# Eight experts of a mixture layer: one store for seven outputs, one load for six inputs

## The chip, the cores and the metric

The kernel runs on one core of a Trainium2 chip. The metric is the device time of one execution in microseconds (us), as the median of repeated runs. A profile is a record of one execution by the hardware profiler; its span runs from the first to the last instruction and is a little shorter than the time of that execution.

Five engines run side by side and wait for each other on semaphores: TensorE (PE in the profile, with PEld for its weight loads), VectorE (DVE), ScalarE (ACT), GpSimd (POOL) and SyncE (SP). Transfers between the chip's memory (DRAM) and the on-chip memory (SBUF) are issued by an engine and carried out by 16 DMA engines.

## What is computed

Each of 8 experts has an input of 256 rows and two weight matrices. The inputs and outputs are float32.

```python
n_experts, capacity, hidden, expert_hidden = 8, 256, 512, 2048
x:  (n_experts, capacity, hidden)
w1: (n_experts, hidden, expert_hidden)
w2: (n_experts, expert_hidden, hidden)

def reference(x, w1, w2):
    h = np.matmul(x, w1)
    h = np.maximum(h, 0)
    return np.matmul(h, w2).astype(np.float32)
```

A weight matrix is 4.19 MB in DRAM, so the sixteen of them are 67.1 MB; all of x is 4.19 MB, and so is the output.

## The kernel before

**Transfers.** Weights, and x of experts 2 to 7, are loaded by DMAs that POOL issues and that cast from float32 to bfloat16 on the way (`load_w1`, L80; `load_w2`, L84; `load_x`, L72). x of experts 0 and 1 is loaded by SP as float32 and cast by VectorE (`load_x_first`, L65). Each of the two weight pools has four buffers, so an expert's weights can only be loaded once the weights of the expert four places before have been used. A weight matrix is one DMA, but for those in `PIECES` (L55): w2 of expert 6 comes in two halves, w2 of expert 7 in a half and two quarters. x of experts 2 and 3, of 4 and 5 and of 6 and 7 come in one load each (`X_GROUPS`, L61), into the two buffers of `xb2`, so that the third waits until expert 3 has been transposed.

**Computation of one expert.** `prepare` (L114) transposes x on TensorE, 8 blocks of 128 by 128, and VectorE copies the result out of PSUM. `layer1` (L127) multiplies with w1 in 64 matmuls of 128x128 by 128x256; ScalarE applies the maximum with 0 after every 8 of them. `layer2` (L149) multiplies with w2 in 32 matmuls of 128x128 by 128x512, into two PSUM tiles, which VectorE copies to the output tile. For an expert in `PIECES` the loop over the rows of w2 is the outer one, so that the first matmuls need only the first piece; for the others the two halves of the output rows come one after the other. The last copy of expert 7 is on ScalarE.

**Stores.** The outputs are gathered in groups (`GROUPS`, L58). `store` (L91) writes a group with one DMA from POOL: experts 0 to 2 in the middle of the kernel, experts 3 to 6 (`DEFER`, L60) just ahead of the second layer of expert 7. Expert 7 is stored from SP (L174), after its last copy.

**Order.** TensorE and POOL run in the order in which the program is written (L178). POOL's is: w1 of 0, identity matrix, w2 of 0, the identity matrix a second time (L184), x of 2 and 3, then w1 and w2 by turns, with x of 4 and 5 behind w2 of 2, and x of 6 and 7 behind w2 of 4. At the end of the list w1 of 7 is put ahead of w2 of 6 (L104). `issue` (L106) only decides at which place of the program a load is written; on POOL that sets the order among loads and stores. The first store stands behind w1 of 7 and ahead of w2 of 6 (L192 to L194). TensorE's order is, for each expert, first layer, transposes of the next expert, second layer; in the last round the first layer of expert 7 comes ahead of the second layer of expert 6 (L197).

The trace shows POOL's issues running ahead of the transfers: eight are in flight, and the ninth is issued at 15.32 us, when the first weights have landed.

Of the kernel before, what the change touches and what calls it, by code (L numbers as in the profile page):

```python
# [10 lines left out]
BF16 = mybir.dt.bfloat16  # L11
# [3 lines left out]
def kernel(  # L15
# [7 lines left out]
    nc = tc.nc  # L23
    P = 128
    E, C, H = x.shape
    F = w1.shape[2]
    MC = C // P
    K1 = H // P
# [5 lines left out]
    xg_v = x.rearrange("e (p mo) k -> p e (mo k)", mo=MC)  # L34
# [4 lines left out]

    const = ctx.enter_context(tc.tile_pool(name="const", bufs=1))  # L40
    x_pool = ctx.enter_context(tc.tile_pool(name="x_pool", bufs=2))
    xb_pool = ctx.enter_context(tc.tile_pool(name="xb_pool", bufs=2))
    xT_pool = ctx.enter_context(tc.tile_pool(name="xT_pool", bufs=2))
    w1_pool = ctx.enter_context(tc.tile_pool(name="w1_pool", bufs=4))
    w2_pool = ctx.enter_context(tc.tile_pool(name="w2_pool", bufs=4))
# [6 lines left out]
    identity = const.tile([P, P], BF16, name="identity")  # L52


    PIECES = {E - 2: [8, 8], E - 1: [8, 4, 4]}  # L55


    GROUPS = [(0, 1, 2), (3, 4, 5, 6), (7,)]  # L58
    GROUP = {e: g for g in GROUPS for e in g}
    DEFER = GROUPS[-2]  # L60
    X_GROUPS = [(2, 3), (4, 5), (6, 7)]  # L61

    xbs, w1s, w2s, outs = {}, {}, {}, {}

    def load_x_first(e):  # L65
        t = x_pool.tile([P, MC * H], FP32, name="x_sb")
        nc.sync.dma_start(t[:], x_v[e])
        b = xb_pool.tile([P, MC, P, K1], BF16, name="xb")
        nc.vector.tensor_copy(b[:].rearrange("p m q k -> p (m q k)"), t[:])  # L69
        xbs[e] = b[:]  # L70

    def load_x(g):  # L72
        t = xb_pool.tile([P, 2, MC, P, K1], BF16, name="xb2")
        nc.gpsimd.dma_start(  # L74
            t[:].rearrange("p e m q k -> p e (m q k)"), xg_v[:, g[0]:g[0] + 2, :]
        )
        for i, e in enumerate(g):
            xbs[e] = t[:, i]
# [5 lines left out]
    def load_w2(e):  # L84
        w2s[e] = t = w2_pool.tile([P, K2 * H], BF16, name="w2_sb")
        k = 0
        for n in PIECES.get(e, [K2]):
            nc.gpsimd.dma_start(t[:, k * H:(k + n) * H], w2_v[e, :, k * H:(k + n) * H])  # L88
            k += n

    def store(g):  # L91
        nc.gpsimd.dma_start(  # L92
            og_v[:, g[0]:g[-1] + 1, :], outs[g][:].rearrange("p e m h -> p e (m h)")
        )

    loads = []
    for e in range(E):
        for g in X_GROUPS:  # L100
            if g[0] == e + 1:
                loads.append((load_x, g))
        loads += [(load_w1, e), (load_w2, e)]
    loads[-3], loads[-2] = loads[-2], loads[-3]  # L104

    def issue(upto):  # L106
        while loads:
            f, e = loads[0]
            if (f, e) not in upto:
                break  # L110
            loads.pop(0)
            f(e)

    def prepare(e):  # L114
        xb = xbs[e]
        xt_ps = psum_t.tile([P, K1, MC, P], BF16, name="xt_ps")
        for ko in range(K1):
            for mo in range(MC):
                nc.tensor.transpose(xt_ps[:, ko, mo, :], xb[:, mo, :, ko], identity[:])  # L119
        xT = xT_pool.tile([P, K1, C], BF16, name="xT")  # L120
        nc.vector.tensor_copy(  # L121
            xT[:].rearrange("p k c -> p (k c)"),
            xt_ps[:].rearrange("p k m q -> p (k m q)"),
        )
        return xT

    def layer1(e, xT):  # L127
        w1_r = w1s[e][:].rearrange("p (ko q j) -> p ko q j", ko=K1, j=K2)
        hT = hT_pool.tile([P, K2, C], BF16, name="hT")
        for pr in range(K2 // 2):  # L130
            h_ps = psum_h.tile([P, 2, C], FP32, name="h_ps")
            for s in range(2):
                j = pr * 2 + s
                for ko in range(K1):
                    nc.tensor.matmul(  # L135
                        h_ps[:, s, :],
                        w1_r[:, ko, :, j],
                        xT[:, ko, :],
                        start=(ko == 0),
                        stop=(ko == K1 - 1),  # L140
                    )
            nc.scalar.activation(  # L142
                hT[:, pr * 2:pr * 2 + 2, :].rearrange("p a c -> p (a c)"),
                h_ps[:].rearrange("p a c -> p (a c)"),
                mybir.ActivationFunctionType.Relu,
            )
        return hT

    def layer2(e, hT):  # L149
        last = e == E - 1  # L150
        g = GROUP[e]
        if e == g[0]:
            outs[g] = out_pool.tile([P, len(g), MC, H], FP32, name=f"out_sb{g[0]}")
        out_sb = outs[g][:, e - g[0]]
        o_ps = [psum_o.tile([P, H], FP32, name="o_ps") for _ in range(MC)]
        if e in PIECES:
            order = [(k, m) for k in range(K2) for m in range(MC)]
        else:
            order = [(k, m) for m in range(MC) for k in range(K2)]
        for k, m in order:  # L160
            nc.tensor.matmul(  # L161
                o_ps[m][:],
                hT[:, k, m * P:(m + 1) * P],
                w2s[e][:, k * H:(k + 1) * H],
                start=(k == 0),
                stop=(k == K2 - 1),
            )
            if k == K2 - 1:
                if last and m == 1:
                    nc.scalar.copy(out_sb[:, m, :], o_ps[m][:])  # L170
                else:
                    nc.vector.tensor_copy(out_sb[:, m, :], o_ps[m][:])  # L172
        if last:
            nc.sync.dma_start(out_v[e], out_sb.rearrange("p m h -> p (m h)"))  # L174

    load_x_first(0)
    load_x_first(1)
    with tc.manual_schedule(engines={mybir.EngineType.PE, mybir.EngineType.Pool}):  # L178
        f, e = loads.pop(0)
        f(e)  # L180
        make_identity(nc, identity)
        f, e = loads.pop(0)
        f(e)
        make_identity(nc, identity)  # L184
        issue([(load_w2, 0), (load_x, X_GROUPS[0]), (load_w1, 1), (load_w2, 1), (load_w1, 2)])
        xT = prepare(0)
        for e in range(E - 1):
            issue(
                [(load_w2, e + 2), (load_w1, e + 3), (load_w1, E - 1), (load_w2, e + 1)]
                + [(load_x, g) for g in X_GROUPS if g[0] <= e + 4]  # L190
            )
            for g in GROUPS[:-2]:  # L192
                if g[-1] == e - 1:
                    store(g)  # L194
            hT = layer1(e, xT)
            xT = prepare(e + 1)
            if e == E - 2:  # L197
                hT_last = layer1(E - 1, xT)
            layer2(e, hT)
        store(DEFER)  # L200
        layer2(E - 1, hT_last)
# [1 line left out]
_INS = ['x', 'w1', 'w2']  # L203
_OUTS = [((8, 256, 512), 'float32')]
# [25 lines left out]
```

## Time and profile before

| what | value |
|---|---|
| median of 5 runs | 182.54 us (182.26 to 182.87) |
| the profiled execution | 182.26 us |
| its span | 180.5 us |
| mean granted TensorE clock | 0.949 |
| read from memory / written to it | 71.30 MB / 4.19 MB |
| share of the packets of POOL's queue (q0) in 16 engines' span | 97.6% |
| TensorE idle ahead of first-layer matmuls, waiting for weights | 35.8 us |
| TensorE idle ahead of second-layer matmuls, waiting for weights | 9.1 us |
| POOL's wait for a free x buffer | 26.4 us |
| POOL's wait of the second store for VectorE's copy | 37.7 us |

The GB/s of the profile count bytes as they are written, so that a weight counts half of what is read. The chain of waits lists the work that ended last in order of time: start, duration, engine and what it computes. `h_ps L135` is a first layer, `o_ps L161` a second layer, `xt_ps L119` the transposes.

When TensorE starts again after a wait for weights, these have just landed. The starts in the trace:

| expert | first layer starts | second layer starts |
|---|---|---|
| 0 | 15.07 | 24.77 |
| 1 | 37.99 | 47.67 (no wait) |
| 2 | 57.41 | 67.04 |
| 3 | 79.22 | 88.96 |
| 4 | 98.62 | 108.82 |
| 5 | 120.50 | 130.16 |
| 6 | 139.85 | 158.74, second half 163.60 |
| 7 | 150.21 | 168.47 |

A first layer takes 7.21 us at the full clock; where TensorE had been idle for 4.57 us or more it took 8.88 to 9.35 us, and the clock that the profile shows fell to half meanwhile.

### The profile page before, as it was taken

The numbers are of one execution on the slowest core, as the hardware profiler recorded it, in microseconds if no ns is written. First come the engines' busy times: TensorE is split into PE (matmuls) and PEld (weight loads), VectorE is DVE, ScalarE is ACT, GpSimd is POOL, SyncE is SP. The second block draws the span as 40 slices with busy tenths as digits, with TensorE's granted clock in tenths as the row PEclk, the third lists the DMA queues.
The fourth block names the chain that finished last, engine by engine and source line by source line (L and its number), as shares of the span: only waits on it lengthen the run. The fifth ranks groups of instructions, "written<-read, shape, count | busy, mean of one in ns | idle before, by whom it ended". The sixth has DMA issues, their size and how long they took to land.

```text
span 180.5 us, 1859 instructions
## 1 busy us (share of the span) xinstructions
PE 125.9 (70%) x832; PEld 89.0 (49%) x832; DVE 17.1 (9%) x25; ACT 40.1 (22%) x66; POOL 15.3 (8%) x32
## 2 busy tenths in 40 slices
PE   0206999059994959449994958629994967887790
PEld 0105964049742944138842954228841967833330
DVE  1300011100111011100111010200111010000210
ACT  2001630014400730005500640004500553600000
POOL 7601011010000031000200002010100000000100
PEclk9999999957999999957999999997999999999998
DMA  6999999999999989989998999999899989999995
GB/s 235 230 232 192 214 232 211 196 232 232 196 211 232 229 167 244 232 174 232 232 229 178 232 193 221 225 232 229 182 229 232 218 189 365 218 214 215 209 390 213
DMA packets 4919, 40.48 MB, mean 224 GB/s; under 512 B 432, under 2 KB 432, under 8 KB 2736
## 3 DMA queue, kind: packets, MB, share of 16 engines
q0 software_dynamic: 4480, 38.80, 97.6%
q1 hardware_dynamic: 432, 1.57, 2.3%
q8 instruction: 6, 0.10, 0.2%
q14 instruction: 1, 0.01, 0.0%
HBM read 71.30 MB, written 4.19 MB: 418 GB/s over the span
## 4 chain that ended last, share of the span: by engine, by line
PE 60%; DMA 19%; another core or an unknown queue 16%; POOL 1%; issue 1%; ACT 0%; POOLq 0%
PE h_ps L135 31%; PE o_ps L161 27%; DMA w_sb<-in_w_dram 19%; PE xt_ps L119 1%; POOL xb L74 0%; POOL w_sb L82 0%; ACT out_sb L170 0%; POOL identity masks.py:199 0%; POOL identity masks.py:197 0%; POOL w_sb L88 0%; POOLq masks.py:199 0%; POOLq L214 0%
## 5 line engine op out<-in xcount | busy, mean ns | idle before, releaser
L135 PE MATMUL h_ps<-xT,w_sb 128*128 128x256 bf16 x512 | 65.2, 294 | 35.8 <-DMA w_sb<-in_w_dram 35.8
L135 PEld LDWEIGHTS <-w_sb 128*128 128x128 bf16 x512 | 60.0, 148 | 42.5 <-DMA w_sb<-in_w_dram 39.1
L142 ACT ACTIVATE hT<-h_ps 128x512 bf16<-128x512 f32 x64 | 38.2, 597 | 117.8 <-PE h_ps L135 117.8
L161 PE MATMUL o_ps<-w_sb,hT 128*128 128x512 bf16 x256 | 56.7, 379 | 9.1 <-DMA w_sb<-in_w_dram 9.1
L161 PEld LDWEIGHTS <-hT 128*128 128x128 bf16 x256 | 25.0, 98 | 38.8 <-issue 10.5
L172 DVE COPY out_sb<-o_ps 128x512 f32<-128x512 f32 x15 | 10.3, 691 | 65.1 <-PE o_ps L161 65.1
L121 DVE COPY xT<-xt_ps 128x1024 bf16<-128x1024 bf16 x8 | 5.5, 690 | 89.3 <-PE xt_ps L119 89.3
L88 POOL DMA_DIRECT2D w_sb<-in_w_dram x11 | 5.9, 536 | 57.9 <-DMA w_sb<-in_w_dram 56.2
L119 PE MATMUL xt_ps<-identity,xb 128*128 128x128 bf16 x64 | 5.3, 230 | 4.8 <-DVE xb L69 4.8
L82 POOL DMA_DIRECT2D w_sb<-in_w_dram x8 | 4.7, 584 | 31.5 <-PE h_ps L135 18.4
L119 PEld LDWEIGHTS <-xb 128*128 128x128 bf16 x64 | 4.7, 117 | 4.7 <-DVE xb L69 4.7
L92 POOL DMA_DIRECT2D out_dram<-out_sb x2 | 1.5, 756 | 37.9 <-DVE out_sb L172 37.7
L170 ACT COPY out_sb<-o_ps 128x512 f32<-128x512 f32 x1 | 0.6, 585 | 17.5 <-PE o_ps L161 17.5
L74 POOL DMA_DIRECT2D xb<-in_x_dram x3 | 2.1, 716 | 26.4 <-PE xt_ps L119 26.4
L69 DVE CAST xb<-x_sb 128x1024 bf16<-128x1024 f32 x2 | 1.4, 698 | 4.5 <-DMA x_sb<-in_x_dram 4.5
L142 ACT ACT_TABLE_LOAD x1 | 1.3, 1283 | 0.7 <-PEq L214 0.7
masks.py:199 POOL TENSOR_SCALAR_AFFINE_SELECT identity<-identity 128x128 bf16<-128x128 bf16 x2 | 0.6, 287 | 0.2
masks.py:197 POOL MEMSET identity<- 128x128 bf16 x2 | 0.4, 224 | 0.0
L214 POOL MEMSET const-float32-0.0<- 128x1 f32 x1 | 0.1, 98 | 0.2 <-issue 0.2
L214 POOL MEMSET const-bfloat16-1.0<- 128x1 bf16 x1 | 0.1, 101 | 0.0
L214 POOL MEMSET const-uint8-127<- 128x1 uint8 x1 | 0.1, 101 | 0.0
L214 POOL MEMSET const-float32-1.0<- 128x1 f32 x1 | 0.1, 98 | 0.0
## 6 DMA issues: line engine op xcount, KB each, us to landing
w_sb<-in_w_dram POOLq DMA_DIRECT2D x14, 2048.0 KB, 61.2
w_sb<-in_w_dram POOLq DMA_DIRECT2D x3, 1024.0 KB, 57.2
out_dram<-out_sb POOLq DMA_DIRECT2D x1, 2048.0 KB, 9.8
xb<-in_x_dram POOLq DMA_DIRECT2D x3, 512.0 KB, 45.4
out_dram<-out_sb POOLq DMA_DIRECT2D x1, 1536.0 KB, 64.4
x_sb<-in_x_dram SPq DMA_DIRECT2D x2, 512.0 KB, 3.6
w_sb<-in_w_dram POOLq DMA_DIRECT2D x2, 512.0 KB, 46.6
out_dram<-out_sb SPq DMA_DIRECT2D x1, 512.0 KB, 3.4
```

Of the source, the lines that this page charges most:

```text
L69: nc.vector.tensor_copy(b[:].rearrange("p m q k -> p (m q k)"), t[:])
L74: nc.gpsimd.dma_start(t[:].rearrange("p e m q k -> p e (m q k)"), xg_v[:, g[0]:g[0] + 2, :])
L82: nc.gpsimd.dma_start(w1s[e][:], w1_v[e])
L88: nc.gpsimd.dma_start(t[:, k * H:(k + n) * H], w2_v[e, :, k * H:(k + n) * H])
L92: nc.gpsimd.dma_start(og_v[:, g[0]:g[-1] + 1, :], outs[g][:].rearrange("p e m h -> p e (m h)"))
L119: nc.tensor.transpose(xt_ps[:, ko, mo, :], xb[:, mo, :, ko], identity[:])
L121: nc.vector.tensor_copy(xT[:].rearrange("p k c -> p (k c)"), xt_ps[:].rearrange("p k m q -> p (k m q)"),)
L135: nc.tensor.matmul(h_ps[:, s, :], w1_r[:, ko, :, j], xT[:, ko, :], start=(ko == 0), stop=(ko == K1 - 1),)
L142: nc.scalar.activation(hT[:, pr * 2:pr * 2 + 2, :].rearrange("p a c -> p (a c)"), h_ps[:].rearrange("p a c -> p (a c)"), mybir.ActivationF ...
L161: nc.tensor.matmul(o_ps[m][:], hT[:, k, m * P:(m + 1) * P], w2s[e][:, k * H:(k + 1) * H], start=(k == 0), stop=(k == K2 - 1),)
L170: nc.scalar.copy(out_sb[:, m, :], o_ps[m][:])
L172: nc.vector.tensor_copy(out_sb[:, m, :], o_ps[m][:])
```

## The change

x of experts 2 to 7 is loaded in one DMA, behind w2 of expert 0, into a buffer of its own; the pool of these tiles has one buffer per name. The first seven outputs form one group, which is stored behind the second layer of expert 6. Loads go by turns to the end: w1 of 6, w2 of 6, w1 of 7, w2 of 7. w2 of expert 6 is one DMA, w2 of expert 7 two halves, and so expert 6 takes the other loop order in its second layer. The first layer of expert 7 stands behind the second layer of expert 6 and the store. The identity matrix is made once.

```diff
-    xb_pool = ctx.enter_context(tc.tile_pool(name="xb_pool", bufs=2))
+    xb_pool = ctx.enter_context(tc.tile_pool(name="xb_pool", bufs=1))
...
-    PIECES = {E - 2: [8, 8], E - 1: [8, 4, 4]}
+    PIECES = {E - 1: [8, 8]}
...
-    GROUPS = [(0, 1, 2), (3, 4, 5, 6), (7,)]
+    GROUPS = [tuple(range(E - 1)), (E - 1,)]
     GROUP = {e: g for g in GROUPS for e in g}
-    DEFER = GROUPS[-2]
-    X_GROUPS = [(2, 3), (4, 5), (6, 7)]
+    X_GROUPS = [tuple(range(2, E))]
...
-        b = xb_pool.tile([P, MC, P, K1], BF16, name="xb")
+        b = xb_pool.tile([P, MC, P, K1], BF16, name=f"xb{e}")
...
     def load_x(g):
-        t = xb_pool.tile([P, 2, MC, P, K1], BF16, name="xb2")
+        t = xb_pool.tile([P, len(g), MC, P, K1], BF16, name="xbs")
         nc.gpsimd.dma_start(
-            t[:].rearrange("p e m q k -> p e (m q k)"), xg_v[:, g[0]:g[0] + 2, :]
+            t[:].rearrange("p e m q k -> p e (m q k)"), xg_v[:, g[0]:g[-1] + 1, :]
         )
...
-    loads[-3], loads[-2] = loads[-2], loads[-3]
...
         make_identity(nc, identity)
-        f, e = loads.pop(0)
-        f(e)
-        make_identity(nc, identity)
         issue([(load_w2, 0), (load_x, X_GROUPS[0]), (load_w1, 1), (load_w2, 1), (load_w1, 2)])
         xT = prepare(0)
         for e in range(E - 1):
             issue(
-                [(load_w2, e + 2), (load_w1, e + 3), (load_w1, E - 1), (load_w2, e + 1)]
+                [(load_w2, e + 2), (load_w1, e + 3), (load_w2, e + 1)]
                 + [(load_x, g) for g in X_GROUPS if g[0] <= e + 4]
             )
-            for g in GROUPS[:-2]:
-                if g[-1] == e - 1:
-                    store(g)
             hT = layer1(e, xT)
             xT = prepare(e + 1)
-            if e == E - 2:
-                hT_last = layer1(E - 1, xT)
             layer2(e, hT)
-        store(DEFER)
-        layer2(E - 1, hT_last)
+        store(GROUPS[0])
+        hT = layer1(E - 1, xT)
+        layer2(E - 1, hT)
```

## The prediction

> **What bounds the kernel now.** I read the page's engine shares first, then its DMA rows, then the chain of waits with its times, then the windows of the last ten microseconds.
>
> ```profile
> PE 125.9 (70%) x832; PEld 89.0 (49%) x832; DVE 17.1 (9%) x25; ACT 40.1 (22%) x66; POOL 15.3 (8%) x32
> DMA  6999999999999989989998999999899989999995
> out_dram<-out_sb POOLq DMA_DIRECT2D x1, 2048.0 KB, 9.8
> out_dram<-out_sb POOLq DMA_DIRECT2D x1, 1536.0 KB, 64.4
> out_dram<-out_sb SPq DMA_DIRECT2D x1, 512.0 KB, 3.4
> ```
>
> TensorE idles for 30% of the span, the DMA engines only in the last slice. So the kernel is a stream of bytes with a tail, and only three things can move its end: the length of the stream, what is left after the last weights, and how well the tail is filled.
>
> ```profile
> 130.16 7.07 PE o_ps L161 x32
> 137.23 2.58 another core or an unknown queue
> 139.81 0.05 issue
> 139.85 7.21 PE h_ps L135 x64
> 147.06 0.45 PE xt_ps L119 x8
> ...
> 150.21 7.21 PE h_ps L135 x64
> 157.42 1.27 another core or an unknown queue
> ...
> 158.74 3.61 PE o_ps L161 x16
> ...
> 163.60 3.61 PE o_ps L161 x16
> ...
> 168.47 7.08 PE o_ps L161 x32
> ```
>
> The "unknown queue" pieces are waits for weights, as the page's groups name them for these lines, so each start after one dates a landing: w2 of expert 5 at 130.16, w1 of 6 at 139.85, w1 of 7 at 150.21, the halves of w2 of 6 at 158.74 and 163.60, the first half of w2 of 7 at 168.47. Starts that lie one whole weight apart (57.41 to 67.04, 79.22 to 88.96, 88.96 to 98.62, 120.50 to 130.16, 130.16 to 139.85 in the same view) give 9.63 to 9.74, mean **9.68 us a weight**; a half takes 4.86 or 4.87. The last quarter so lands near 168.47 + 4.87 = 173.34.
>
> ```profile
> 170.00:171.00 1.00, 1.00 (x6) 0.47 (x5) 0.00 (x0) 0.00 (x0) 0.00 (x0) 1.00 1.00 201
> 171.00:172.00 1.00, 1.00 (x7) 0.47 (x5) 0.00 (x0) 0.00 (x0) 0.00 (x0) 1.00 1.04 266
> 173.00:174.00 1.00, 1.00 (x6) 0.49 (x5) 0.00 (x0) 0.00 (x0) 0.00 (x0) 1.00 1.06 434
> 174.00:175.00 1.00, 1.00 (x7) 0.45 (x5) 0.00 (x0) 0.00 (x0) 0.00 (x0) 1.00 0.99 410
> 175.00:176.00 1.00, 0.54 (x3) 0.04 (x1) 0.64 (x1) 0.43 (x1) 0.00 (x0) 1.00 1.03 426
> 176.00:177.00 1.00, 0.00 (x0) 0.00 (x0) 0.05 (x1) 0.16 (x1) 0.00 (x0) 1.00 0.72 295
> 178.00:179.00 1.00, 0.00 (x0) 0.00 (x0) 0.00 (x0) 0.00 (x0) 0.00 (x0) 1.00 0.56 229
> ```
>
> The last number is GB/s written. With the three windows left out (348, 410, 12) the ten add to 3.03 MB after 170.0; the two stores in there are 2.62 MB, so 0.41 MB is weights, 1.92 us at the 213 of the windows before. The store phase therefore starts at **171.93**, runs at a mean of 423 in its middle, and ends where 229 runs out, 178.0 + 229/423 = 178.54, call it 178.57 with the last 12. Without loss it would have ended at 171.93 + 2.62/0.423 = 178.12; most of the 0.45 lost is the window of 295, (423 - 295)/423 = 0.30: the big store runs dry and the last one, issued at 176.19, is not yet flowing. The last store lands at 176.19 + 3.40 = 179.59, 1.02 after its bytes; 0.91 later the span ends.
>
> **The change, part by part.**
>
> *The store of experts 0 to 2 leaves the stream.* From w1 of 6 to the first half of w2 of 6 it is 158.74 - 139.85 = 18.89 us; less w1 of 7 (9.68) and the half (4.86) leaves 4.35 for this store, 362 GB/s for its 1.573 MB. At the 423 of the tail it would be 3.72. The last weights land 4.35 us earlier (3.72 at least, if its turnarounds stay), at 168.99.
>
> *It comes back in the tail.* 3.67 MB go out behind the last weights, and 0.52 MB from SP: 4.194 MB / 0.423 = 9.92 us from 171.93 - 4.35 = 167.58, so until 177.50. The trace has 3 us of unbroken store, not 9; the bounds are 423 there and 362 in mid-stream. I take 423, as this store too is followed by no loads. Together the two edits give 3.72 - 4.35 = -0.63.
>
> The Trainium skill speaks against this part: "DMA: Bandwidth & Descriptors", section "Where 436 GB/s comes from", says that HBM to SBUF transfers are bound at about 358 GB/s by the memory's side. By it the 4.194 MB take an estimated 11.7 us and the kernel gets about 0.7 us slower; the windows of 434, 410 and 426 lie above that figure, so I go by them.
>
> *The dip closes.* The last store now joins while the big one still flows. The 0.30 of the window 176 to 177 goes: -0.30 (0 if something else makes the dip).
>
> *The order of w1 of 7 and w2 of 6; first layer of 7 behind the second of 6 on TensorE; halves for w2 of 7, none for 6.* Equal bytes: 0 for the stream. The landings become 149.53 (w2 of 6), 159.21 (w1 of 7), 164.1 and 168.99 (halves of w2 of 7). TensorE: second layer of 6 from 149.53 for 7.07 to 156.60; idle 2.61; first layer of 7 from 159.21 for 7.21 to 166.42; second layer of 7 for 7.07, its later half needed at 166.47 + 3.54 = 170.0, 1.0 after it lands, so no stall; end 173.54. By the 0.65 between 175.54 and SP's issue now, the last store is issued at 174.2, alone it lands at 177.6, and the span would end at 178.5. That is 1.0 before the bytes allow, so it is hidden under the big store. Without that cover TensorE's tail would set 178.5.
>
> *The big store's wait* on the VectorE copy of expert 6 ends near 157.3. Nothing stands behind it on POOL, and its ring is busy with weights until 167.58: 0.
>
> *The x load of 3.15 MB instead of three of 1.05.* In the landings x of 4 and 5 cost 67.04 to 79.22 less 9.68 = 2.50, x of 6 and 7 (98.62 to 120.50 less two weights) 2.52, x of 2 and 3 (24.77 to 37.99 less one) 3.54. The one load costs between 3 x 2.50 = 7.5 and the sum, 8.56; the position is that of the dear one, so I take the sum: 0 (down to -1.0). It lands w1 of expert 1 about 5.0 us later. Later experts regain that as 2.5 and 2.5 vanish from the stream, and TensorE has 2 us of idle time a weight to follow; from expert 5 on nothing is later than now. If the cover went, at most one half-clocked first layer (9.35 for 7.21) would be late there, long before the end.
>
> *Five DMAs fewer (24 to 19 on POOL), no wait for an xb buffer (26.4), one identity less (0.66).* In the trace a weight in halves takes 9.73 against 9.68 whole, so a transfer more costs 0.05; five are 0.25 at most, of which I count nothing. POOL issues eight transfers ahead: the latest issue, at 130.40, lands over 40 us later. The new w1 and w2 waits for buffers end some 60 us before their bytes are due. All 0.
>
> The skill's "DMA: Bandwidth & Descriptors", section "Anatomy of one DMA", puts a fixed 2.0 us on each transfer; in series five fewer would be an estimated 10 us. The halves contradict it for a full queue.
>
> **Sum.** -0.63 - 0.30 = -0.93: span 180.5 to 179.57, this execution 182.26 to 181.33. It was the fastest of five, 0.28 under the median of 182.54, so the forecast is **181.6 us**. Open: the receipt at the end. SP's bytes took 1.02 to land; the 2 MB store landed at 178.42, between 0.9 and 1.9 after its bytes, depending on where in the dip they ended. If the big store is last and slow, up to 0.9 comes back (-0.03); if x saves its 1.0 and receipt is quick, -1.9. Own range of the forecast 180.7 to 182.1.
>
> **The rivals.**
>
> *Bytes are bytes.* The DMA engines move the same sum, and losses of 0.63 and 0.30 were only shifted or are eaten by the slower receipt: 182.3 to 182.8. For it: the DMA row is full. Against it: the 362 and 295 are losses that are seen. A variant ends there too: the clock halves in the 2.61 us before the first layer of 7. That layer then takes 9.35, the last store is issued at 176.3, just as the big one has drained (167.58 + 3.67/0.423 = 176.26), and lands at 179.7, as now. Five idle times of 2.55 to 2.67 kept the clock, 4.57 and more halved it. Chance 0.18.
>
> *Slower: a long store runs at the mid-stream rate.* Place: the tail after the last weights. Price: 4.194/0.362 = 11.59 against 6.64 + 4.35 = 10.99 available before, +0.60: 183.1. It decides below 4.194/10.99 = 382 GB/s. For it: the only row of a Pool store longer than its end effects shows 362. Against it: loads on both sides of that one. Chance 0.23.
>
> *The change does not shorten the stream*, because the store issued mid-kernel was filling holes that the loads leave: then the last weights land hardly earlier and the end comes some 3 us later. The DMA row has no holes there; chance 0.02, counted with the slower ones.
>
> **How the numbers follow.** Forecast 0.57, no change 0.18, slower 0.25. This kernel's runs tell no more than about 0.2%, 0.37 us, from no change. The range 180.8 to 183.2 holds most of the forecast's own range, all of the second case, and the third to just past its 183.1.
>
> **What would show it.** Right: last weights 4.3 us earlier on the second layer of 7, about 10 us of windows at 410 to 430 GB/s behind them without a dip, the last store issued near 174.2 and the big one landing last. Wrong: windows near 360 there; a first layer of 7 over 9 us; a last weight less than 3.7 us earlier.

## The result and the profile after

The changed kernel takes 182.01 us (median of 30 runs, 181.75 to 182.84) where the kernel before took 182.41 (median of 54): a ratio of 0.998, 95% interval 0.9974 to 0.9987. Timed again later it was 181.95 against 182.36, 0.9979 (0.9970 to 0.9988). Three executions, the profiled ones of order_only and split_sp among them, took 268 to 338 us; the ratios and profiles used here leave them out. The direction and the range of the prediction held, but the gain is 0.4 us where 0.93 was worked out. In the profiled executions it is 182.26 to 181.69, in the span 180.5 to 179.9.

The last two stores on the page of the changed kernel, with size and time from issue to landing:

```profile
out_dram<-out_sb POOLq DMA_DIRECT2D x1, 3584.0 KB, 20.0
out_dram<-out_sb SPq DMA_DIRECT2D x1, 512.0 KB, 3.6
```

POOL issues its store at 157.76 and SP at 175.46, so POOL's lands at 177.76 and SP's at 179.06: the small store is the last, not the big one as forecast. Before, it landed at 179.59. (The page gives the time to landing to a tenth, so a landing worked out from it, here and below, is good to some 0.05 us.) The end of the chain of waits (start, duration, what):

```profile
149.67 7.07 PE o_ps L158 x32
156.73 2.58 another core or an unknown queue
159.31 0.05 issue
159.36 8.55 PE h_ps L132 x64
167.91 6.92 PE o_ps L158 x32
174.83 0.02 issue
174.85 0.58 ACT out_sb L167
```

w2 of 6 has landed at 149.67 and w1 of 7 at 159.36 (worked out: 149.53 and 159.21). The first layer of 7 takes 8.55 instead of 7.21: the granted clock fell to 0.50 in the wait ahead of it and was back at 1.00 only from 163. So the last store is issued 1.26 later than worked out. The windows of the tail, the last number being GB/s written:

```profile
166.00:167.00 1.00, 1.00 (x12) 1.00 (x11) 0.00 (x0) 0.60 (x1) 0.00 (x0) 1.00 0.99 205
167.00:168.00 1.00, 1.00 (x11) 0.87 (x10) 0.00 (x0) 0.65 (x2) 0.00 (x0) 1.00 0.87 225
168.00:169.00 1.00, 1.00 (x6) 0.45 (x5) 0.00 (x0) 0.54 (x1) 0.00 (x0) 1.00 0.95 352
169.00:170.00 1.00, 1.00 (x6) 0.49 (x5) 0.00 (x0) 0.00 (x0) 0.00 (x0) 1.00 1.07 442
...
175.00:176.00 1.00, 0.00 (x0) 0.00 (x0) 0.33 (x1) 0.44 (x1) 0.00 (x0) 1.00 1.01 418
176.00:177.00 1.00, 0.00 (x0) 0.00 (x0) 0.00 (x0) 0.00 (x0) 0.00 (x0) 1.00 1.04 426
177.00:178.00 1.00, 0.00 (x0) 0.00 (x0) 0.00 (x0) 0.00 (x0) 0.00 (x0) 1.00 0.76 307
178.00:179.00 1.00, 0.00 (x0) 0.00 (x0) 0.00 (x0) 0.00 (x0) 0.00 (x0) 1.00 0.22 90
```

With the windows between (401, 430, 422, 418, 426) this is 4.56 MB after 166.0. The stores are 4.19, the 0.37 left are weights, 1.73 us at 213 GB/s. The store phase starts at **167.73** (worked out: 167.58) and holds 423 GB/s for eight windows: the long store is as fast as the short one. Without loss it would end at 167.73 + 4.194/0.423 = 177.65; its bytes run out at 178 + 90/423 = **178.21**. Before, it was 178.12 and 178.57. The tail lost 0.45 us then and loses 0.56 now: the dip of the window of 295 has gone, but a window of 307 has come at 177. These ends of the bytes are means over the DMA engines. By the packet records of the trace the last packet of SP's store ends later, at 179.28 before and at 178.70 now, and the store has landed 0.34 us after it in both.

### The profile page after: what moved, and what is told of

Read it like the earlier page. It is cut to its first block, busy times and chain, and to the rows that moved or that the text cites. A ratio compares the mean times of both kernels' runs of the same rounds, so it can differ in the third digit from the quotient of the medians.

```text
span 179.9 us, 1852 instructions
## 1 busy us (share of the span) xinstructions
PE 127.5 (71%) x832; PEld 89.9 (50%) x832; DVE 17.4 (10%) x25; ACT 40.1 (22%) x66; POOL 11.8 (7%) x25
## 3 DMA queue, kind: packets, MB, share of 16 engines
HBM read 71.30 MB, written 4.19 MB: 420 GB/s over the span
## 4 chain that ended last, share of the span: by engine, by line
PE 56%; DMA 27%; another core or an unknown queue 12%; POOL 2%; issue 1%; ACT 0%; POOLq 0%
PE h_ps L132 27%; PE o_ps L158 27%; DMA w_sb<-in_w_dram 27%; PE xt_ps L116 1%; POOL w_sb L81 1%; POOL xbs L73 0%; ACT out_sb L167 0%; POOL w_sb L87 0%; POOL identity masks.py:199 0%; POOL identity masks.py:197 0%; POOLq masks.py:199 0%; POOLq L204 0%
## 5 line engine op out<-in xcount | busy, mean ns | idle before, releaser
L132 PE MATMUL h_ps<-xT,w_sb 128*128 128x256 bf16 x512 | 67.0, 299 | 36.1 <-DMA w_sb<-in_w_dram 36.1
L132 PEld LDWEIGHTS <-w_sb 128*128 128x128 bf16 x512 | 60.9, 148 | 44.0 <-DMA w_sb<-in_w_dram 39.8
L87 POOL DMA_DIRECT2D w_sb<-in_w_dram x9 | 5.1, 562 | 42.5 <-PE o_ps L158 23.9
L81 POOL DMA_DIRECT2D w_sb<-in_w_dram x8 | 4.4, 556 | 48.2 <-PE h_ps L132 38.0
L116 PE MATMUL xt_ps<-identity,xb 128*128 128x128 bf16 x16 | 1.6, 264 | 4.9 <-DVE xb L68 4.9
L91 POOL DMA_DIRECT2D out_dram<-out_sb x1 | 0.9, 940 | 55.8 <-DVE out_sb L169 55.8
L116 PEld LDWEIGHTS <-xb 128*128 128x128 bf16 x16 | 1.3, 127 | 4.9 <-DVE xb L68 4.9
L116 PE MATMUL xt_ps<-identity,xbs 128*128 128x128 bf16 x48 | 3.7, 219 | 0.0
L116 PEld LDWEIGHTS <-xbs 128*128 128x128 bf16 x48 | 3.3, 113 | 0.0
L73 POOL DMA_DIRECT2D xbs<-in_x_dram x1 | 0.8, 837 | 0.0
```

Of the source, the lines that this page charges most:

```text
L73: nc.gpsimd.dma_start(t[:].rearrange("p e m q k -> p e (m q k)"), xg_v[:, g[0]:g[-1] + 1, :])
L81: nc.gpsimd.dma_start(w1s[e][:], w1_v[e])
L91: nc.gpsimd.dma_start(og_v[:, g[0]:g[-1] + 1, :], outs[g][:].rearrange("p e m h -> p e (m h)"))
L132: nc.tensor.matmul(h_ps[:, s, :], w1_r[:, ko, :, j], xT[:, ko, :], start=(ko == 0), stop=(ko == K1 - 1),)
```

## The experiments

In the tables "SP lands" and "POOL lands" are the issue of each queue's last store plus its time to landing. Theory A: the recorded sum holds, and the late first layer of expert 7 keeps the rest of the gain back. B: the bytes set the end, and they gain less. D came from the first four runs: a last store on POOL's queue ends the kernel later than one on SP's. C, E and F are explained in the expectations that name them.

### The change taken apart

Store alone: the kernel before with one group.

```diff
-    GROUPS = [(0, 1, 2), (3, 4, 5, 6), (7,)]
+    GROUPS = [tuple(range(E - 1)), (E - 1,)]
```

> The kernel before with one edit: experts 0 to 6 are one group, stored behind the last weights; x, the order of the loads and of TensorE, and the pieces stay. Theory A (the recorded sum is right, and the changed kernel falls short of it because its last store is issued late, after a first layer of expert 7 that ran 8.55 us at the half clock instead of 7.21): here that layer is done long before its second layer's weights, the last store is issued near 171.8 us, and the span falls by 0.8 to 1.0 us (ratio 0.995). Theory B (the bytes: taking the store out of the stream is worth less than the 0.63, and the dip nothing more): the span falls by 0.4 like the changed kernel's (ratio 0.998).

x alone: `X_GROUPS`, the sizes in `load_x` and the pool as in the diff of the change, nothing else.

> The kernel before with one edit: x of experts 2 to 7 in one load behind the first w2, in a buffer of its own. Theory A and theory B: no change (ratio 1.000, within 0.1%), with the first layer of expert 1 starting about 5 us later than 37.99 and that of expert 6 at 139.85. Theory C (the x load is what costs the missing part of the gain): 0.2 to 0.5 us slower (ratio 1.001 to 1.003), the first layer of expert 6 starting that much later.

Order alone:

```diff
-    PIECES = {E - 2: [8, 8], E - 1: [8, 4, 4]}
+    PIECES = {E - 1: [8, 8]}
...
-    loads[-3], loads[-2] = loads[-2], loads[-3]
...
-            if e == E - 2:
-                hT_last = layer1(E - 1, xT)
...
-        layer2(E - 1, hT_last)
+        hT = layer1(E - 1, xT)
+        layer2(E - 1, hT)
```

> The kernel before with only the order changed: w1 of 6, w2 of 6, w1 of 7, w2 of 7; first layer of 7 behind the second of 6; halves for w2 of 7, none for 6. Stores and x loads stay as they were. In the recorded working this order costs nothing because the big store covers it. Without that cover: w1 of 7 lands at 163.6, first layer to 170.8 (172.1 at the half clock), second to 177.9 (179.2), last store issued at 178.5 (179.9): the span is 182.8 (184.1), 2.3 to 3.6 us longer than before (ratio 1.013 to 1.020). If TensorE's tail did not matter at all, ratio 1.000.

Store and x without the order:

> The kernel before with the one store of seven outputs and the one x load, but with its own order and pieces: the change without the order. Theory A (the recorded sum: 0.93 gained, and the order at best costs): span 179.5, ratio 0.995. Theory D (a POOL store that lands last ends the kernel some 1.65 us after its landing, an SP store some 0.85 after; so the store in one loses 0.3 as long as TensorE is early, and the change's order helps by making SP's store the last): SP's store issued near 171.6, POOL's lands last near 178.8, span 180.3 to 180.8, ratio 1.000 to 1.002, slower than the changed kernel by 0.3 to 0.8 us.

Store and order without x:

> The change without the x load: three x loads as before. Theory D with the 0.3 us that x_only gained: the span is 0.2 to 0.4 us longer than the changed kernel's, ratio 0.999 to 1.000. Theory A (x costs nothing and brings nothing): the ratio of the changed kernel, 0.998.

| kernel | median us | ratio to before (95% interval) |
|---|---|---|
| store_only | 182.69 | 1.0025 (1.0010 to 1.0040) |
| x_only | 182.11 | 0.9988 (0.9979 to 0.9998) |
| order_only | 183.90 | 1.0084 (1.0068 to 1.0100) |
| store_and_x | 182.79 | 1.0021 (1.0009 to 1.0033) |
| store_and_order | 181.89 | 0.9971 (0.9960 to 0.9983) |

The parts don't add. The store alone, the core of the recorded sum, makes the kernel 0.3 to 0.45 us slower; the order alone makes it 1.5 slower; store and order together make it 0.4 to 0.5 faster. Both A and B are wrong on store_only. D's time for store_and_x came out, but not the landings it gave: SP's store landed last, at 179.47, and POOL's at 178.92. x alone gained 0.2 to 0.3, which no theory had forecast, but added to the store it changed nothing (1.0025 and 1.0021), and without it the rest is no slower, where D had expected 0.2 to 0.4 us.

### Why the store alone loses

The stores of store_only on its page:

```profile
out_dram<-out_sb POOLq DMA_DIRECT2D x1, 3584.0 KB, 14.0
out_dram<-out_sb SPq DMA_DIRECT2D x1, 512.0 KB, 6.9
```

Issued at 165.15 and 171.94, they land at 179.15 (POOL) and 178.84 (SP). SP's store is 0.75 us earlier than in the kernel before and yet the span ends at 180.8, 1.65 after POOL's landing. Two more kernels test this. In the first, expert 7 is stored from POOL, and nothing else is changed:

```diff
-            nc.sync.dma_start(out_v[e], out_sb.rearrange("p m h -> p (m h)"))
+            nc.gpsimd.dma_start(out_v[e], out_sb.rearrange("p m h -> p (m h)"))
```

> The kernel before with the store of expert 7 issued from POOL instead of SP, otherwise the same. Theory D: the landing comes up to 0.4 us later (POOL's issue takes 0.76 for 0.35), and the span ends 1.6 us after it instead of 0.9: 0.8 to 1.2 us slower, ratio 1.004 to 1.007. Without a dearer end on POOL's queue: 0 to 0.4 us, ratio 1.000 to 1.002.

It took 183.10 us against 182.36, 1.0043 (1.0031 to 1.0056). Its store is issued at 176.68 and lands in 3.0, at 179.68, hardly later than SP's 179.59 in the kernel before; the span ends at 181.5, 1.82 later. What happens in between is in the view of the line that launches the kernel (L225), where POOL's queue waits at the end for its transfers (count; shortest, median and longest in ns; first and last start):

```profile
L225 POOLq DRAIN  x3: 45/87/4096, 176.7 to 181.2; - x3
```

The longest drain starts with the issue and ends at 176.7 + 4.10 = 180.8, 1.1 after the landing; the other engines' last steps follow. For store_and_x the same view has

```profile
L225 POOLq DRAIN  x3: 45/93/12819, 167.0 to 180.3; - x3
```

so a drain until 167.0 + 12.8 = 179.8, 0.9 after POOL's landing at 178.92, and 0.8 ahead of the end of the span, as in before_pool_last. So POOL's queue ends this kernel too, although SP's store lands last.

In the second kernel the bytes of store_and_x are shared out differently:

```diff
-    GROUPS = [(0, 1, 2), (3, 4, 5, 6), (7,)]
+    GROUPS = [tuple(range(E - 3)), tuple(range(E - 3, E))]
...
-    DEFER = GROUPS[-2]
+    DEFER = GROUPS[0]
...
-            nc.sync.dma_start(out_v[e], out_sb.rearrange("p m h -> p (m h)"))
+            nc.sync.dma_start(
+                og_v[:, g[0]:g[-1] + 1, :], outs[g][:].rearrange("p e m h -> p e (m h)")
+            )
```

> As store_and_x (before's order, one x load), but POOL's store behind the last weights holds experts 0 to 4 only, and SP stores experts 5, 6 and 7 together as soon as expert 7 is done: the same bytes in the tail, in another share of the two queues. Theory D: POOL's store lands near 177.0, SP's last near 178.9, span 179.6 to 179.8, 0.6 us or more below store_and_x, ratio 0.996 to 0.998. Theory B (bytes alone): no difference to store_and_x.

> split_sp once more, for its profile. Theory D: POOL's store of experts 0 to 4 lands near 177 and its drain ends a microsecond later, SP's 1.57 MB land last near 179.0, span 179.7 to 180.1. If instead POOL's lands last here too, the 0.8 us between split_sp and store_and_x have another cause.

182.01 us, 0.9980 (0.9970 to 0.9990), against 182.79 for store_and_x on the same chip: 0.8 us from another share of the same bytes. In the profile (split_p1) SP's last store lands at 179.24, POOL's at 175.49, earlier than the 177 expected.

Not all of this is the end of the queue. The two profiles differ by 0.5 us in the span, and 0.2 of it is SP's earlier landing. POOL's store is issued at 167.02 in store_and_x and at 130.99 in split_p1, and behind the last weights the DMA engines ran partly empty in store_and_x alone (its window first, then that of split_p1; the last two numbers are the busy share of the DMA engines and GB/s):

```profile
168.00:169.00 1.00, 1.00 (x6) 0.48 (x5) 0.00 (x0) 0.00 (x0) 0.00 (x0) 1.00 0.63 193
168.00:169.00 1.00, 1.00 (x7) 0.44 (x5) 0.00 (x0) 0.00 (x0) 0.00 (x0) 1.00 1.01 352
```

In store_only, with the store issued at 165.15, this window has 1.01 and 360, which fits a store that was issued too late in store_and_x; no run tests that alone. The other 0.3 us of the two profiles is the longer end behind POOL's store.

| kernel | SP lands | POOL lands | span | span less SP's | span less POOL's |
|---|---|---|---|---|---|
| before | 179.59 | 178.42 | 180.5 | 0.91 | 2.08 |
| changed | 179.06 | 177.76 | 179.9 | 0.84 | 2.14 |
| split_p1 | 179.24 | 175.49 | 180.1 | 0.86 | 4.61 |
| store_only | 178.84 | 179.15 | 180.8 | 1.96 | 1.65 |
| store_and_x | 179.47 | 178.92 | 180.6 | 1.13 | 1.68 |
| before_pool_last | none | 179.68 | 181.5 | none | 1.82 |

The span ends some 0.9 us after SP's landing or some 1.7 after POOL's, whichever is later. By the completion times in the trace, which are finer than the table, it is 0.87 or 0.88 after SP's in all fifteen profiles in which SP's decides. D holds, by before_pool_last above all, where nothing but the queue was changed. By this sum POOL's store decides once it lands less than 0.8 ahead of SP's; in the changed kernel it is 1.3 ahead.

### Does TensorE's late tail hold the gain back?

First ten matmuls more, meant to keep the clock up:

```diff
         store(GROUPS[0])
+        warm = psum_h.tile([P, 2, C], FP32, name="h_ps")
+        for _ in range(10):
+            nc.tensor.matmul(
+                warm[:].rearrange("p a c -> p (a c)"), hT[:, 0, :P],
+                w2s[E - 2][:, :H], start=True, stop=True,
+            )
         hT = layer1(E - 1, xT)
```

> The changed kernel with ten matmuls more (128x128 by 128x512, into a PSUM tile that nothing reads) between the second layer of expert 6 and the first of expert 7, where TensorE waits 2.62 us for weights. Theory A: the clock stays at full speed there, the first layer of 7 takes 7.2 instead of 8.55, the last store is issued near 174.1 instead of 175.46, and the time falls below that of the changed kernel by 0.3 to 0.5 us (ratio to the kernel before 0.995 to 0.996). Theory B: the layer gets faster but the end is set by the bytes; the ratio stays at 0.998.

181.88 us, 0.9979 (0.9966 to 0.9992), which tells little: the second layer of 6 ran 8.75 us in its profile, the ten matmuls started only at 158.31, the first layer of 7 took 7.15 but began at 160.46, and SP's store was issued at 175.17. The next kernel leaves out half of the first layer of expert 7:

```diff
-        for pr in range(K2 // 2):
+        for pr in range(K2 // 4 if e == E - 1 else K2 // 2):
...
-                hT[:, k, m * P:(m + 1) * P],
+                hT[:, k % 8 if last else k, m * P:(m + 1) * P],
```

> The changed kernel with half of the first layer of expert 7 left out (32 of 64 matmuls; the second layer uses the other half twice). TensorE's tail ends 2 us or more earlier, SP's last store is issued near 173.2 instead of 175.46. Theory A (the late tail sets the end): 0.3 to 0.6 us faster than the changed kernel, ratio 0.995 to 0.996. Theory B (the bytes alone): no difference to it, 0.998. Theory D: with less work it gets slower, because POOL's big store is now the last to land (near 178.7): span 180.3 to 180.5, ratio 1.000 to 1.001.

181.85 us, 0.9971 (0.9960 to 0.9983), an interval that overlaps the changed kernel's 0.9974 to 0.9987; on the page of this kernel the last store is

```profile
out_dram<-out_sb SPq DMA_DIRECT2D x1, 512.0 KB, 5.7
```

It is issued at 173.36, 2.1 us earlier than in the changed kernel, and lands at 179.06, where it landed there. POOL's lands at 178.11, so D's forecast that POOL's would be last missed. The packet records show what held SP's store up: its first packet starts at 176.20, 2.8 us after the issue, and until then POOL's store had the DMA engines to itself. In the changed kernel it starts at 176.32, 0.9 after the issue. A falls: TensorE's half-clock layer did not delay the landing.

### Is the dip a loss that can be had back?

The kernel before without the last 4 of the 32 matmuls in the second layer of expert 7, so that its last store is issued slightly earlier:

```diff
+        n_k = K2 - 2 if last else K2
         for k, m in order:
+            if k >= n_k:
+                break
...
-                stop=(k == K2 - 1),
+                stop=(k == n_k - 1),
             )
-            if k == K2 - 1:
+            if k == n_k - 1:
```

> The kernel before, with the last two of the 16 slices of the second layer of expert 7 left out (4 of 32 matmuls), so that SP's last store is issued near 175.3 instead of 176.19, with unchanged loads and stores. If the dip of the window 176 to 177 is a loss that can be had back (recorded term): no dip, and 0.2 to 0.4 us faster, ratio 0.998 to 0.999. If the loss only moves to the end of the tail, because the DMA engines run out unevenly, or POOL's store then lands last: no dip, a ragged last window, ratio 1.000 to 1.002.

182.36 us against 182.36, 1.0008 (0.9994 to 1.0021). Its tail:

```profile
175.00:176.00 1.00, 0.00 (x0) 0.00 (x0) 0.09 (x1) 0.20 (x1) 0.00 (x0) 1.00 1.02 422
176.00:177.00 1.00, 0.00 (x0) 0.00 (x0) 0.00 (x0) 0.00 (x0) 0.00 (x0) 1.00 1.03 422
177.00:178.00 1.00, 0.00 (x0) 0.00 (x0) 0.00 (x0) 0.00 (x0) 0.00 (x0) 1.00 0.83 340
178.00:179.00 1.00, 0.00 (x0) 0.00 (x0) 0.00 (x0) 0.00 (x0) 0.00 (x0) 0.91 0.35 143
```

The dip has gone (422 where 295 stood), a ragged end of 340 and 143 has come, and the store issued at 175.23 takes 4.3 and lands at 179.53, against 179.59 for one issued 0.96 later. The loss only moves.

The completion records of the trace show how. A store's completion comes in sixteen steps, as many as there are DMA engines, so I take each step for one engine. In the kernel before, ten steps of the last store come from 178.64 to 178.81 and six from 179.32 to 179.62. In before_early ten come from 177.87 to 178.38 and six from 179.12 to 179.51. POOL's store lands in the same two groups, its last six steps 1.23 or 1.24 us ahead of those of SP's in both kernels, and 1.24 us is what a sixteenth of SP's store takes at a sixteenth of 423 GB/s. So the earlier store filled the time of the engines that had run out of work; the six that are behind still had POOL's share to finish and then SP's, and they set the landing. The last weights of the kernel before land in the same way, ten steps up to 172.27 and six from 173.09 to 173.34. Why six are behind is open.

Without any cover the same store is shorter still, as the second run of the order alone shows:

> order_only once more, for its profile. Its median was 1.5 us above the kernel before, where 2.3 to 3.6 were expected without the big store's cover. If TensorE's tail sets the end: SP's store is issued near 177.7 and lands 3.4 us later, the span ends 0.85 after that, with DMA windows empty for a microsecond ahead of it. The missing 0.8 to 2 us then show in the landings: w1 of 7 nearer 163 than 163.6.

```profile
176.00:177.00 1.00, 1.00 (x6) 0.43 (x5) 0.00 (x0) 0.00 (x0) 0.00 (x0) 1.00 0.72 295
177.00:178.00 1.00, 0.61 (x3) 0.10 (x1) 0.57 (x1) 0.35 (x1) 0.00 (x0) 1.00 0.21 86
178.00:179.00 1.00, 0.00 (x0) 0.00 (x0) 0.12 (x1) 0.23 (x1) 0.00 (x0) 1.00 0.00 0
179.00:180.00 1.00, 0.00 (x0) 0.00 (x0) 0.00 (x0) 0.00 (x0) 0.00 (x0) 1.00 0.93 381
```

Here the DMA engines are empty for a microsecond; SP's store, issued at 178.26, lands 2.6 us later, at 180.86, with its sixteen steps within 0.18 us, and the span ends at 181.8. That is the order's own price, TensorE's tail with nothing over it. w1 of 7 landed at 163.49, where 163.6 was worked out, so the landings are not what made it smaller than the 2.3 to 3.6 expected; it is that the last store alone takes 2.6, not the 3.4 that I had read off the kernel before, where the big one was still in the way.

### Is the store's price in mid-stream real, and does x matter?

> The kernel before, profiled once more. Theory F (the recorded 4.35 us for the store in mid-stream is what it usually costs): from the start of the first layer of 6 to the second layer of 6 it is 18.8 to 19.0 us again. Theory E (it is usually less, as the 18.39 in x_only suggests, where this store is the same): 18.3 to 18.5, so the store costs 3.8 to 3.9 and taking it out gains 0.1 instead of the recorded 0.63.

From the first layer of 6 to the second it is 139.80 to 159.13 = 19.33 us here, above even F's range. By the longer way from the first layer of 5, less three and a half weights (33.90), the store costs 4.34 in the kernel before, 4.82 here, 3.92 in x_only and 4.18 in before_early, 4.3 in the mean. E falls, and the recorded 4.35 stands as a mean, with 0.9 us between the lowest and the highest.

> The changed kernel, profiled once more. Theories E and D: SP's last store lands last, near 179.1, POOL's a microsecond earlier, span 179.8 to 180.3. Theory A: a first layer of 7 at the full clock, if this execution has one (7.2 for 8.55), moves the end forward by as much as SP's issue, 0.5 us or more.

> The changed kernel again, beside store_and_order_r. All theories: ratio 0.997 to 0.999.

> The change without the x load, again. If the x load in one gains what x_only showed (0.2 to 0.3 us), this is slower than after_r by that. If it does nothing for the end, both have the same ratio within 0.1%. If it costs, this is faster, as the 0.9971 of the first run of it would have it.

The changed kernel's SP store landed at 179.16 and 179.48 in these two profiles, POOL's at 177.86 and 178.25; the first layer of 7 took 8.85 and 8.88. Side by side on one chip the changed kernel took 181.95 (0.9979, 0.9970 to 0.9988), and without the x load in one 181.90 (0.9975, 0.9964 to 0.9986). x does nothing for the end within the change; the 0.2 to 0.3 us of x_only was measured once, and what made it is open. No kernel here is clearly faster than the changed one.

## Why the prediction was right and wrong

**The stream and the rate: right.** Taking the store out brings the last weights forward about as recorded, by 4.20 us in the first two profiles where 4.35 was worked out. In after_half, where TensorE waits for it, the second half of w2 of 7 lands at 169.10 (worked out 168.99). The long store holds 423 GB/s. So the slower rival, the tail at 362, didn't happen, and neither did what the Trainium skill's 358 GB/s ("DMA: Bandwidth & Descriptors", section "Where 436 GB/s comes from") would have made of it: 401 to 442 were measured here too, in windows of stores alone. In the profiles this term is 1.573/0.423 = 3.72 less 171.93 - 167.73 = 4.20, so -0.48 for the recorded -0.63; the changed kernel's profile also started 0.17 later, as the first weights landed at 15.24 instead of 15.07.

**"The dip closes ... -0.30": wrong, and the step that failed.** The dip did close, and it brought nothing. before_early closes it alone and gains 0.00 us; 0.30 us would be a ratio of 0.9984, outside its interval of 0.9994 to 1.0021. The loss of the tail went from 0.45 to 0.56 us, at its end instead of in its middle. The step took the DMA engines as one. "The big store runs dry" held for ten of its sixteen completion steps, which came from 176.72 to 177.27; the other six came from 178.08 to 178.38, and what was still to be stored there set the end, whether the ten were busy or not. With this term at +0.11 the profiles' sum is -0.48 + 0.11 = -0.37, as the bytes' end shows (178.57 to 178.21). SP's landing came 0.53 earlier in these two profiles, and the medians moved by 0.40. The range held although a third of the sum was wrong, because it was wide; the prediction had itself allowed 0 for this term.

Two readings beside it were wrong too. The receipt of 1.02 for SP's store, and of 0.9 to 1.9 for the big one, is mostly engines that are behind: SP's last packet ends at 179.28, 0.34 before its landing, and POOL's at 178.03, 0.35 before. And the 3.40 us of the last store were taken for its time alone. Alone it takes 2.6; in the kernel before it takes 3.4, or 4.3 when issued earlier, and in the changed kernel 3.6 or 5.7, and in each pair it lands within 0.1 us of the same time. The 3.40 is no term of the sum; it made TensorE's tail without cover 0.8 too long.

**The rival "bytes are bytes" had the better half of the mechanism.** Its sentence that losses might only be shifted is what the dip did. Its variant, the half clock ahead of the first layer of 7, happened too, in the place foreseen (8.55 us; 9.35 was worked out). But the variant let it cost the whole gain, with a landing at 179.7, and after_half shows that it did not delay the landing at all. That five waits of 2.6 us had kept the clock was the luck of one profile: in the second profile of the kernel before, all three first layers behind waits of 2.59 to 2.68 took 8.87 or 8.88.

**"The order: 0" was right in number, wrong in meaning.** It was costed as hidden under the big store, and it is: alone it costs 1.5 us. But it also has POOL's store issued earlier (157.76, against 165.15 in store_only) and SP's later (175.46, against 171.94), so that POOL's is through well before SP's. Without the order the end of POOL's queue sets the end of the kernel, and the change is a loss of 0.4 to 0.5 us (store_and_x; a part of it is the partly empty window). The prediction had this price as an open receipt "up to 0.9" for a slow big store; the runs show it as some 0.8, the difference of the two ends, and not as a matter of the bytes.

**"The big store lands last": wrong.** In all three profiles of the changed kernel SP's lands last, by 1.2 to 1.3 us.

**x, and the DMAs saved: right as far as it shows.** With the one x load the changed kernel took 181.95 us, without it 181.90; what fewer DMAs save was not measured apart.

## What to carry to other kernels

Where the DMA engines are full to the end, the time from issue to landing of the last transfer contains the queue ahead of it: issuing it 1.0 and 2.1 us earlier bought nothing here. What paid, by the sum above, was that the store no longer stands between loads. Before counting a dip in the tail as a gain, close it alone and see whether the end moves: a mean over sixteen DMA engines doesn't show the few that are behind. And look at which queue ends last: the last store on POOL instead of SP, with nothing else changed, cost 0.74 us.

## What the runs showed of the hardware

- The span ended 0.87 or 0.88 us after the landing where SP's store decided (fifteen profiles), and 1.65 to 1.8 after it where POOL's did (three); POOL's queue drained until 0.9 to 1.1 us past its landing.
- Whether waits of 2 to 2.7 us halve the clock differed between executions. In the first profile of the kernel before, all five waits of 2.55 to 2.70 left the layer behind them at the full clock; in its second, none of the three of 2.59 to 2.68 did. In the changed kernel's first profile four of the six layers behind a wait of 2.62 to 2.68 took 8.55 to 8.88. In after_half a second layer behind a wait of 1.99 took 8.75 for 7.07. The Trainium skill, "TensorE: Matmul & The Clock Gate", section "Part 1: The HAM clock gate", has the clock drop after an idle window of about 3.4 us; the waits here are shorter than that.
- A 0.52 MB store took 2.6 us with the DMA engines empty and up to 6.9 (store_only) beside a 3.67 MB store of the other queue. It did not share the engines from its issue on: its first packet started 0.8 us after the issue in order_p1, 2.8 in after_half, 3.6 in store_only and 4.1 in store_and_x.
- Sixteen completion steps of one transfer came in two groups, ten and then six, with 0.5 us between the groups in the last stores of the kernel before and of the changed one; in order_p1, with the engines empty, all came within 0.18 us.
